# One layer of a hybrid diffusion model on one core: fewer gathers ticked in the latent finish, and its transposes queued later

## The chip, the core and the metric

The kernel runs on one core of a Trainium2 chip. TensorE (PE) multiplies matrices, with its weight loads listed as PEld; VectorE (DVE) and ScalarE (ACT) do the elementwise work, GpSimd (POOL) issues the indirect DMAs and a little arithmetic, and SyncE (SP) issues the plain loads and stores. The metric is the device time of one execution in microseconds, as the median of the runs.

## The reference

One layer is computed for 256 context tokens and 1024 latent tokens of width 1024. Attention and a recurrent mixer run side by side; their outputs go through one output projection and a gated residual, then a norm, and the result goes to an expert retrieval (PEER) with 16384 experts, of which every token takes 16 in each of 8 heads:

```python
    mix = jnp.concatenate([o_att, o_rnn.astype(o_att.dtype)], axis=-1)
    x = x + ga1 * jnp.einsum('bsm,md->bsd', mix, w_out)
    h2 = modulated_norm(x, g_ffn, sh2, sc2)
    x = x + ga2 * peer(h2, pq, psk, pu, pv)
...
        u = jnp.take(u_tab, eid, axis=0)
        act = jax.nn.gelu(jnp.einsum('td,thkd->thk', xb, u).astype(jnp.float32))
        vv = jnp.take(v_tab, eid, axis=0)
        return jnp.einsum('thk,thkd->td', (g * act).astype(vv.dtype), vv)
```

A final norm of every token ends it.

## The kernel before, in words

The tokens are ten tiles of 128: two of context, eight latent. The experts of six latent tiles are computed **densely**: every one of 128 groups of 128 experts is multiplied for all 768 tokens (the products u, lines 138 to 140), and what the retrieval did not choose is multiplied by zero. The other four tiles, two of context and two latent, take their experts by **gathers** in `mix` (lines 848 to 884): for each of a tile's 128 choices, POOL gathers 128 rows of `peer_u` (line 859) and DVE takes the dot product with the token (line 862), and for each again POOL gathers 128 rows of `peer_v` (line 873) and DVE adds them, weighted, to `acc` (line 879). One such step, called a row here, moves 128 by 1024 numbers of 4 bytes, 0.524 MB, and there are 1024 of them. A row waits for a free buffer: four serve it everywhere, three more in the dense part alone.

The stages run in this order: modulations and the context; the context's retrieval beside the latent projections, the recurrence and the rotation of queries and keys (lines 330 to 334); the latent attention, which begins with keys and queries cut in two halves (lines 398 to 414) for the scores (line 431); the latent **finish**, which is the output projection, residual and norm, tile by tile (lines 485 to 548); the **choose**, which finds the latent tiles' experts; the **spread**, in 96 blocks, which lays the chosen weights out over all experts (lines 697 to 706) while PE computes the u products of 44 groups ahead of the dense part ("early", 2112 matmuls of 384 columns); the **dense** part; and the last tiles' `final` (lines 835 to 845).

The rows are put between the other work by a clock. `tick(us)` is called after a piece of work and adds its microseconds; each time the clock has gone past a step the next row is emitted. The step is `F_STEP`, 1.9, up to the spread (others in some phases; none at all is emitted in the spread by its own tick), and `D_STEP`, 2.05, in the dense part. A scheduler then sets each engine's order from the place of emission and a simulated time of its own, so that a row can stand earlier than it was emitted, in any gap that it sees. In the dense part this is shut out: there each row's work is tied behind an add of that part (`paced`).

In the finish, `x` holds a tile's residual stream. Per tile PE makes two products of 512 columns (line 526, eight matmuls each), DVE multiplies by the gate and adds (lines 528 and 529), x is stored, ACT squares it (line 535), the root is taken with a step on POOL (lines 145 to 151), ACT scales x (line 537), and `to_columns` transposes it on PE (line 248) into the columns hh and hl that the experts' products take. In tiles that are gathered, f is transposed back (line 545) and stored.

## Time and profile before

| what | us |
|---|---|
| runs, median (lowest to highest of 3) | 3565.87 (3563.97 to 3566.43) |
| the profiled execution | 3568.34 |
| its span | 3566.5 |
| context, modulations | 0 to 365 |
| latent projection, recurrence, rotation, the context's retrieval | 245 to 534 |
| latent attention | 534 to 706 |
| latent finish | 706 to 887 |
| choose | 887 to 1177 |
| spread | 1222 to 1619 |
| what is left of the early products | 1619 to 1702 |
| dense part, to PE's last product | 1712 to 3521 |
| tail | 3521 to 3566.5 |

The stage's borders are read from the first and last instructions of its lines; stages overlap at them. The mean granted clock of the execution is 0.955 of full speed. A window's line gives each engine's busy time in it, with the number of instructions; a wait's line gives the time that an engine stood idle and the instruction whose end let it go on.

### The profile page before, as it was taken

The page shows a single profiled execution, that of the slowest core. Times are in us where ns is not written, and L with a number is a line of the kernel's source. Part 1 is how long each engine was busy: PE and PEld are TensorE (multiplying, and loading weights), DVE is VectorE, ACT ScalarE, POOL GpSimd, SP SyncE. Part 2 cuts the span into 40 slices and gives each one's busy share as a digit, 9 for nine tenths or more (in the row PEclk, how much of TensorE's full clock was granted, in tenths as well). Part 3 has the DMA queues.
Part 4 walks back from the last instruction along what each step waited for, and adds up shares of the span by engine and source line. Part 5 has one row for each costly group of instructions (what it writes and reads, how often), then busy time and mean ns, then how long its engine had stood idle before and what let it go on. Part 6 is the DMA issues. An engine that isn't in the chain of part 4 may idle for free.

```text
span 3566.5 us, 48580 instructions
## 1 busy us (share of the span) xinstructions
PE 3210.4 (90%) x16982; PEld 2704.1 (76%) x16982; DVE 3111.0 (87%) x6762; ACT 1429.9 (40%) x2242; POOL 1716.4 (48%) x1146
## 2 busy tenths in 40 slices
PE   7788868777999888888899999999999999999994
PEld 4477645433889877778788888878888887888884
DVE  4649989877999999993599999989999998999998
ACT  5734647523112344433333334333334333333432
POOL 0012451466521223443266666656666655666665
PEclk9799989988999999999999999999999999999997
DMA  8342652588621367795699999989999998999996
GB/s 331 136 152 82 216 206 83 185 276 290 219 89 31 122 199 214 233 315 185 242 325 337 337 330 334 340 308 335 329 328 339 327 340 290 332 327 336 335 339 223
DMA packets 349141, 918.19 MB, mean 257 GB/s; under 512 B 29144, under 2 KB 150104, under 8 KB 345824
## 3 DMA queue, kind: packets, MB, share of 16 engines
q0 software_dynamic: 147456, 536.94, 42.9%
q1 hardware_dynamic: 201440, 378.16, 30.8%
q8 instruction: 133, 2.18, 0.2%
q14 instruction: 112, 0.92, 0.1%
HBM read 834.48 MB, written 80.50 MB: 257 GB/s over the span
## 4 chain that ended last, share of the span: by engine, by line
PE 43%; DVE 22%; issue 8%; DMA 8%; POOL 3%; ACT 2%; SPq 0%; POOLq 0%; DVEq 0%; ACTq 0%
PE u L138 6%; PE u L140 6%; PE u L139 6%; PE rot L138 5%; PE rot L140 5%; PE rot L139 5%; DVE acc L879 3%; DVE row L862 3%; DMA row<-in_peer_u,eid 2%; PE res L138 2%; PE res L139 2%; PE res L140 2%; DMA row<-in_peer_v,eid 2%; DMA ad<-a 2%; DVE oh L699 1%
## 5 line engine op out<-in xcount | busy, mean ns | idle before, releaser
L859 POOL DMA_INDIRECT row<-in_peer_u,eid x512 | 749.9, 1465 | 603.3 <-DVE acc L879 201.7
L873 POOL DMA_INDIRECT row<-in_peer_v,eid x512 | 719.9, 1406 | 583.6 <-DVE acc L879 283.7
L138 PE MATMUL u<-hh,uh 128*128 128x384 f32 x2048 | 707.1, 345 | 22.4 <-ACT a L1028 22.4
L140 PE MATMUL u<-hh,ul 128*128 128x384 f32 x2048 | 705.6, 345 | 4.7 <-DVE ul L135 4.7
L139 PE MATMUL u<-hl,uh 128*128 128x384 f32 x2048 | 707.1, 345 | 0.0
L879 DVE SCALAR_TENSOR_TENSOR acc<-row,w,acc 128x1024 f32<-128x1024 f32 x508 | 663.4, 1306 | 25.2 <-DMA row<-in_peer_v,eid 23.7
L862 DVE SCALAR_TENSOR_TENSOR row<-row,h 128x1024 f32<-128x1024 f32 x512 | 623.0, 1232 | 62.8 <-DMA row<-in_peer_u,eid 62.6
L764 ACT ACTIVATE q<-rot 128x512 f32<-128x512 f32 x504 | 300.0, 597 | 523.5 <-PE rot L140 295.5
L138 PE MATMUL rot<-vh,ah 128*128 128x512 f32 x1024 | 409.1, 400 | 16.6 <-ACT q L764 16.1
L138 PEld LDWEIGHTS u<-hh,uh 128*128 128x128 f32 x2048 | 394.7, 193 | 29.8 <-ACT a L1028 23.8
L140 PEld LDWEIGHTS u<-hh,ul 128*128 128x128 f32 x2048 | 394.2, 192 | 9.7 <-DVE ul L135 5.1
L139 PE MATMUL rot<-vl,ah 128*128 128x512 f32 x1024 | 401.4, 392 | 0.0
L140 PE MATMUL rot<-vh,al 128*128 128x512 f32 x1024 | 400.6, 392 | 0.0
L139 PEld LDWEIGHTS u<-hl,uh 128*128 128x128 f32 x2048 | 394.6, 193 | 4.5
L765 DVE TENSOR_TENSOR acc<-q,acc 128x512 f32<-128x512 f32 x504 | 341.8, 686 | 45.4 <-ACT q L764 42.3
L140 PE MATMUL mm<-hh,wl 128*128 128x256 f32 (+2 forms) x848 | 289.7, 342 | 9.8 <-POOL wl L135 6.9
L138 PE MATMUL mm<-hh,wh 128*128 128x256 f32 (+2 forms) x848 | 286.3, 338 | 5.6 <-ACT wh L134 5.6
L139 PE MATMUL mm<-hl,wh 128*128 128x256 f32 (+2 forms) x848 | 284.3, 335 | 0.0
L134 ACT ACTIVATE uh<-u 128x1024 fp32r<-128x1024 f32 x128 | 135.8, 1061 | 331.3 <-PE u L139 302.0
L135 POOL TENSOR_TENSOR ul<-u,uh 128x1024 fp32r<-128x1024 f32 x44 | 122.8, 2791 | 277.8 <-ACT uh L134 237.5
L138 PEld LDWEIGHTS rot<-vh,ah 128*128 128x128 f32 x1024 | 193.4, 189 | 74.9 <-ACT q L764 36.7
L140 PEld LDWEIGHTS rot<-vh,al 128*128 128x128 f32 x1024 | 193.2, 189 | 41.5
(271 smaller groups left out, 5955.3 us busy)
## 6 DMA issues: line engine op xcount, KB each, us to landing
u<-in_ut SPq DMA_DIRECT2D x128, 512.0 KB
v<-in_peer_v SPq DMA_DIRECT2D x128, 512.0 KB
gd<-stg SPq DMA_DIRECT2D x12, 4096.0 KB
gt<-gd SPq DMA_DIRECT2D x64, 768.0 KB
w<-in_w_mod SPq DMA_DIRECT2D x24, 1024.0 KB
ad<-a SPq DMA_DIRECT2D x88, 192.0 KB
a<-ad SPq DMA_DIRECT2D x44, 384.0 KB
w<-in_w_query SPq DMA_DIRECT2D x32, 512.0 KB
```

The costliest lines, as they stand in the source:

```text
L134: A.activation(hi, src, AF.Copy)
L135: return (eng or V).tensor_tensor(lo, src, hi, op=OP.subtract)
L138: T.matmul(out, lhs[0], rhs[0], start=first, stop=False)
L139: T.matmul(out, lhs[0], rhs[1], start=False, stop=False)
L140: T.matmul(out, lhs[1], rhs[0], start=False, stop=last)
L699: V.tensor_tensor(oh.rearrange(four, j=2), o2.rearrange(four, j=2), pairs(gh, ts), op=OP.mult)
L764: A.activation(q, p, AF.Copy)
L765: tick(share / (2 * (N_DENSE - N_RES)), V.tensor_tensor(y, q, y, op=OP.add))
L859: G.indirect_dma_start(out=u, out_offset=None, in_=i["peer_u"], in_offset=bass.IndirectOffsetOnAxis(ap=eid[:, k:k + 1], axis=0))
L862: V.scalar_tensor_tensor(u, u, 1.0, h2, op0=OP.mult, op1=OP.mult, accum_out=act[:, j:j + 1])
L873: G.indirect_dma_start(out=v, out_offset=None, in_=i["peer_v"], in_offset=bass.IndirectOffsetOnAxis(ap=eid[:, k:k + 1], axis=0))
L879: V.scalar_tensor_tensor(acc, v, w[:, j:j + 1], acc, op0=OP.mult, op1=OP.add)
```

## The change

Three things. `D_STEP` goes from 2.05 to 2.0. In the latent finish the tick of 14 us a tile becomes 3 after each product and 2 at the end, 8 in all, so that 8 / 1.9 or about four rows are emitted a tile in the place of 14 / 1.9 or about seven. And a latent tile's norm, from the square to the transposes, moves into a function `normed` that is called after the next tile's products, with the transposes on PE tied behind the last of them (`issue_after`); x gets three buffers for it and f two. The context's finish has the same function without that tie, and its tick of 14 stays; f's second buffer is there too.

```diff
--- before.py
+++ after.py
@@ -51,7 +51,7 @@
 N_MORE = 3
 
 F_STEP = 1.9
-D_STEP = 2.05
+D_STEP = 2.0
 
 AFTER = 90.0
 STEP = {"spread": 1e9, "ret": 4.0, "early": 1.0}
@@ -507,13 +507,34 @@
         wk = pool(es, f"{pre}wk")
         ps = pool(es, f"{pre}po", 2, space=PSUM)
         xs = {}
+
+        def normed(t, x, behind):
+
+            ss = wk.tile([P, 1], F32, name="ss", bufs=2)
+            f = wk.tile([P, KD, P], F32, name="f", bufs=2)
+            A.activation(f.rearrange("p k t -> p (k t)"), x, AF.Square, accum_out=ss)
+            rs = rstd_of(ss, wk)
+            A.activation(x, x, AF.Copy, scale=rs)
+            hh, hl, us = dest(t)
+            with tc.issue_after(behind) if behind else nullcontext():
+                to_columns(ps, f, x, hh, hl, us, a2, b2, cond)
+                if t_0 + t in gt:
+                    h2 = wk.tile([P, D], F32, name="h2")
+                    for kk in range(2):
+                        p = ps.tile([P, 4, P], F32, name="tr")
+                        for k in range(4):
+                            T.transpose(p[:, k], f[:, kk * 4 + k], ident)
+                        A.activation(h2[:, kk * 512:(kk + 1) * 512], p.rearrange("p k t -> p (k t)"), AF.Copy)
+                    nc.sync.dma_start(h2d[t_0 + t], h2)
+
+        waiting = None
         for c0 in range(0, D, HW):
             if c0:
                 weights(c0)
             for t in tiles:
                 ts = slice(t * P, (t + 1) * P)
                 if c0 == 0:
-                    x = wk.tile([P, D], F32, name="x", bufs=2)
+                    x = wk.tile([P, D], F32, name="x", bufs=3 if lat else 2)
                     nc.sync.dma_start(x, x_in[ts, :])
                     xs[t] = x
                 x = xs[t]
@@ -523,29 +544,25 @@
                     p = ps.tile([P, W], F32, name="mm")
                     for k in range(KD):
                         oT = qT[:, k, ts] if k < 4 else gy[:, k - 4, ts]
-                        T.matmul(p, oT, wo[c0][:, k, wc], start=(k == 0), stop=(k == KD - 1))
+                        ins = T.matmul(p, oT, wo[c0][:, k, wc], start=(k == 0), stop=(k == KD - 1))
                     y = wk.tile([P, W], F32, name="y", bufs=2)
                     V.tensor_tensor(y, p, ga1[:, cols], op=OP.mult)
                     V.tensor_tensor(x[:, cols], y, x[:, cols], op=OP.add)
+                    if lat:
+                        tick(3)
                 if c0 + HW < D:
                     continue
                 nc.sync.dma_start(x1d[t_0 + t], x)
-                ss = wk.tile([P, 1], F32, name="ss", bufs=2)
-                f = wk.tile([P, KD, P], F32, name="f")
-                A.activation(f.rearrange("p k t -> p (k t)"), x, AF.Square, accum_out=ss)
-                rs = rstd_of(ss, wk)
-                A.activation(x, x, AF.Copy, scale=rs)
-                hh, hl, us = dest(t)
-                to_columns(ps, f, x, hh, hl, us, a2, b2, cond)
-                if t_0 + t in gt:
-                    h2 = wk.tile([P, D], F32, name="h2")
-                    for kk in range(2):
-                        p = ps.tile([P, 4, P], F32, name="tr")
-                        for k in range(4):
-                            T.transpose(p[:, k], f[:, kk * 4 + k], ident)
-                        A.activation(h2[:, kk * 512:(kk + 1) * 512], p.rearrange("p k t -> p (k t)"), AF.Copy)
-                    nc.sync.dma_start(h2d[t_0 + t], h2)
-                tick(14)
+                if not lat:
+                    normed(t, x, None)
+                    tick(14)
+                    continue
+                if waiting:
+                    normed(*waiting, ins.ins)
+                waiting = t, x
+                tick(2)
+        if waiting:
+            normed(*waiting, None)
 
 
     picks = {}
```

How many rows' work stands on DVE ahead of a place, counted in the order of the two programs:

| ahead of | before | after |
|---|---|---|
| the first cut of the latent queries (line 414) | 48 | 62 |
| the first gate multiply of the latent finish | 98 | 112 |
| the end of the latent finish (start of choose) | 180 | 200 |
| the end of choose | 210 | 223 |
| the first multiply of the dense part | 249 | 223 |
| the last add of the dense part | 1020 | 1012 |
| the program's end | 1024 | 1024 |

The retrieval weights of the two gathered latent tiles are combined on DVE (114 instructions); they stand behind the spread's last block before and inside the spread now. On PE, 414 of the early u products stand behind the last product of the spread before, 596 now.

DVE, the last rotations of the latent queries and keys and the halves of keys and queries that attention needs (kl, qs), before; L862 and L879 are rows:

```order
L332 TENSOR_TENSOR t_4236<-g,sinT 128x512
L862 SCALAR_TENSOR_TENSOR row,act<-row,h_4356 128x1024
L332 TENSOR_TENSOR t_4242<-g,sinT 128x512
L334 TENSOR_TENSOR qT<-qT,t_4236 128x512
L334 TENSOR_TENSOR qT<-qT,t_4242 128x512
L862 SCALAR_TENSOR_TENSOR row,act<-row,h_4356 128x1024
L399 TENSOR_TENSOR kl<-kcT,kh 64x256 x2
L399 TENSOR_TENSOR kl<-kT,kh 64x256 x4
L399 TENSOR_TENSOR kl<-kT,kh 64x512 x2
L414 TENSOR_TENSOR qs<-qT,qs 64x512 x3
```

and after, where rows are on L896 (or L879):

```order
L334 TENSOR_TENSOR qT<-qT,t_4242 128x512
L896 SCALAR_TENSOR_TENSOR acc<-row,w,acc 128x1024
L399 TENSOR_TENSOR kl<-kcT,kh 64x256 x2
L399 TENSOR_TENSOR kl<-kT,kh 64x256
L896 SCALAR_TENSOR_TENSOR acc<-row,w,acc 128x1024
L399 TENSOR_TENSOR kl<-kT,kh 64x256
L896 SCALAR_TENSOR_TENSOR acc<-row,w,acc 128x1024
L399 TENSOR_TENSOR kl<-kT,kh 64x256 x2
L896 SCALAR_TENSOR_TENSOR acc<-row,w,acc 128x1024
L399 TENSOR_TENSOR kl<-kT,kh 64x512 x2
L896 SCALAR_TENSOR_TENSOR acc<-row,w,acc 128x1024 x2
L414 TENSOR_TENSOR qs<-qT,qs 64x512 x4
```

The first qs stands behind 14 more rows in all; five rows have come among the kl, where there were none, and one right ahead of them stayed.

PE in the finish, before; the eight transposes tr are one tile's, mm the products, each product four matmuls with qT and four with gy:

```order
L526 MATMUL mm<-w,qT 128x512 x4
L526 MATMUL mm<-w,gy 128x512 x4
L526 MATMUL mm<-w,qT 128x512 x4
L248 MATMUL tr<-ident,x 128x128 x8
L526 MATMUL mm<-w,gy 128x512 x4
L526 MATMUL mm<-w,qT 128x512 x4
L526 MATMUL mm<-w,gy 128x512 x4
```

and after:

```order
L547 MATMUL mm<-w,qT 128x512 x4
L547 MATMUL mm<-w,gy 128x512 x4
L547 MATMUL mm<-w,qT 128x512 x4
L547 MATMUL mm<-w,gy 128x512 x4
L248 MATMUL tr<-ident,x 128x128 x8
L547 MATMUL mm<-w,qT 128x512 x4
```

A tile's transposes stood between the products of the next tile's second half, and stand behind the last of them now.

POOL at the program's end, before; a DMA row is a gather for the last tile, L147 a step of a final norm's root:

```order
L873 DMA row<-in_peer_v,eid_9939 128x1024 x4
L873 DMA row_31948<-in_peer_v,eid_9939 128x1024
L837 TENSOR_TENSOR acc_16235<-acc_16235,vh 128x1024
L837 TENSOR_TENSOR acc_16237<-acc_16237,vh 128x1024
L147 TENSOR_TENSOR rs_r<-rs_m,nhalf 128x1 x7
L1119 UNCONDITIONAL_BRANCH
```

and after:

```order
L854 TENSOR_TENSOR acc_16153<-acc_16153,vh 128x1024
L854 TENSOR_TENSOR acc_16155<-acc_16155,vh 128x1024
L890 DMA row<-in_peer_v,eid_9858 128x1024 x3
L147 TENSOR_TENSOR rs_r<-rs_m,nhalf 128x1
L890 DMA row<-in_peer_v,eid_9858 128x1024
L147 TENSOR_TENSOR rs_r<-rs_m,nhalf 128x1 x4
L890 DMA row<-in_peer_v,eid_9858 128x1024
L147 TENSOR_TENSOR rs_r<-rs_m,nhalf 128x1
L890 DMA row<-in_peer_v,eid_9858 128x1024
L147 TENSOR_TENSOR rs_r<-rs_m,nhalf 128x1
L1136 UNCONDITIONAL_BRANCH
```

The last six gathers went from ahead of the final norms to behind two tiles' gate multiplies (L854) and between the norms' roots: one root stands ahead of the fourth of them, five ahead of the fifth and six ahead of the last.

## Rows read from the trace of the kernel before

**Rows 1.** Windows: us; busy us (count) PE, PEld, DVE, ACT, POOL; PEclk; DMA; GB/s

```profile
450.00:534.00 84.00, 56.52 (x203) 38.52 (x203) 68.98 (x86) 36.83 (x57) 47.92 (x33) 0.87 0.59 208
...
706.00:887.00 181.00, 133.22 (x343) 64.70 (x344) 131.88 (x196) 54.60 (x105) 114.64 (x90) 0.86 0.83 282
...
887.00:1177.00 290.00, 266.80 (x1647) 255.92 (x1646) 281.86 (x1677) 60.46 (x101) 85.31 (x53) 0.96 0.36 112
...
1222.00:1619.00 397.00, 349.10 (x2813) 308.99 (x2813) 375.92 (x848) 172.87 (x210) 138.48 (x67) 0.95 0.76 232
...
1619.00:1650.00 31.00, 22.50 (x127) 22.18 (x125) 25.09 (x166) 11.74 (x16) 9.93 (x7) 0.89 0.92 286
...
1650.00:1700.00 50.00, 50.00 (x291) 50.00 (x290) 0.00 (x0) 10.64 (x17) 11.98 (x5) 1.00 0.27 90
...
2200.00:2800.00 600.00, 592.73 (x2876) 522.44 (x2876) 568.20 (x729) 230.69 (x350) 384.94 (x258) 0.99 0.91 331
...
3521.00:3566.50 45.50, 0.38 (x2) 0.00 (x0) 39.44 (x57) 11.04 (x20) 15.65 (x10) 0.55 0.39 149
```

**Rows 2.** Waits of PE and DVE, 450 to 535 us: total, times, longest

```profile
PE s L431 <- DVE qs L414: 20.7, 1, 20.7
...
DVE row L862 <- DMA row<-in_peer_u,eid: 6.8, 4, 3.4
```

**Rows 3.** Waits in the latent finish, 706 to 887 us

```profile
ACT x L537 <- DVE rs_r L151: 53.1, 8, 9.5
...
PE tr L248 <- ACT x L537: 46.2, 8, 17.9
...
DVE row L862 <- DMA row<-in_peer_u,eid: 28.0, 20, 4.0
...
DVE acc L879 <- DMA row<-in_peer_v,eid: 15.6, 12, 3.2
```

**Rows 4.** Line 528 in the finish: what DVE waited for before it

```profile
  PE mm L526: 0.5, 1
```

**Rows 5.** Lines of the finish: group | busy us, mean ns | idle before

```profile
L862 DVE SCALAR_TENSOR_TENSOR row<-row,h 128x1024 f32<-128x1024 f32 x43 | 54.3, 1268 | 28.2 <-DMA row<-in_peer_u,eid 28.0
...
L879 DVE SCALAR_TENSOR_TENSOR acc<-row,w,acc 128x1024 f32<-128x1024 f32 x38 | 48.8, 1284 | 16.2 <-DMA row<-in_peer_v,eid 15.6
```

**Rows 6.** Windows, two stretches of the spread

```profile
1250.00:1300.00 50.00, 44.06 (x372) 38.56 (x373) 48.98 (x135) 23.62 (x29) 10.64 (x4) 0.97 0.62 183
...
1500.00:1550.00 50.00, 43.66 (x332) 39.25 (x333) 45.81 (x63) 20.79 (x27) 23.34 (x15) 0.90 0.83 270
```

**Rows 7.** Waits of PE, spread to dense start, 1222 to 1720 us

```profile
PE g L703 <- DVE oh L699: 26.3, 16, 2.1
...
PE u L138 <- ACT a L1028: 17.2, 4, 8.5
...
PE res L138 <- ACT ah L134: 10.5, 1, 10.5
```

**Rows 8.** Waits of PE in the dense part, 1712 to 3525 us

```profile
PE rot L138 <- ACT q L764: 16.1, 9, 5.0
PE res L138 <- ACT ah L134: 14.9, 3, 10.5
```

**Rows 9.** Lines of DVE in the dense part

```profile
L862 DVE SCALAR_TENSOR_TENSOR row<-row,h 128x1024 f32<-128x1024 f32 x384 | 461.5, 1218 | 20.2 <-DMA row<-in_peer_u,eid 20.2
```

**Rows 10.** Timeline of DVE, tail: start us, us, engine, line

```profile
3542.78 1.21 DVE L838 TENSOR_TENSOR h<-acc,h 128x1024 f32<-128x1024 f32 x1
...
3550.11 1.28 DVE L842 SCALAR_TENSOR_TENSOR h<-h,rs_r,row 128x1024 f32<-128x1024 f32 x1
...
3559.95 2.48 DVE L842 SCALAR_TENSOR_TENSOR u<-u,rs_r,vh 128x1024 f32<-128x1024 f32 x2
```

**Rows 11.** Timeline of POOL, tail

```profile
3528.10 5.61 POOL L837 TENSOR_TENSOR acc<-acc,vh 128x1024 f32<-128x1024 f32 x2 [5.32 <-DMA vh<-modd]
...
3553.04 2.79 POOL L147 TENSOR_TENSOR rs_r<-rs_m,nhalf 128x1 f32<-128x1 f32 x2 [2.44 <-DVE rs_m L145]
```

## The prediction

> **What bounds the kernel now.** I read the windows first, by stage, then the waits of the engine that ends each stage, then the lines and the tail's timeline. The reader is to see that no one engine bounds the whole.
>
> Ahead of the latent attention PE stands 20.7 us at one place, until DVE has made the first halves of the queries [rows 2]. DVE is busy 69.0 of 84 us there [rows 1] and waits 6.8 us for gathered rows [rows 2]. DVE's queue is in order, so what stands on it ahead of these halves delays the attention.
>
> In the finish no engine is full: PE 133 of 181 us, DVE 132 [rows 1]. PE's one large wait is 46.2 us for scaled x, in eight pieces, one a tile [rows 3]. It looks like the stage's price and is not: before the gate multiplies, the first work on a tile's product, DVE waited for PE only once, 0.5 us [rows 4]. PE is ahead of DVE in spite of its stalls. DVE itself waits 43.6 us for gathered rows (28.0 and 15.6) [rows 3]. So DVE's in-order queue and the gathers feeding it set the pace: 81 rows in 181 us [rows 5], 2.2 us a row, where one row's work is 1.27 to 1.28 us [rows 5].
>
> Choose is DVE's: 281.9 of 290 us [rows 1]. In the spread both are near full, PE 349 of 397, DVE 376 [rows 1], and PE waits 26.3 us for one-hot tiles of DVE and 17.2 for ACT [rows 7]. What is left of the early products then runs at full PE with an idle DVE: 50.00 and 0.00 of 50 us [rows 1]. From there to the tail PE is the bound: 592.7 of 600 us in the window shown, DVE 568.2 [rows 1]; of its waits none as large as 6 us comes after the 10.5 at the start [rows 8]. The tail is DVE's and a chain: 39.4 of 45.5 us [rows 1].
>
> **The change part by part.** The counts are those of the table of rows ahead of places. The sum is made against the profiled execution, 3568.3 us, which is 2.5 above the median of the runs.
>
> *The way to the attention.* 14 more rows stand ahead of the first qs; 14 x 1.22 us (a row's dot product in the dense part, [rows 9]) is 17. Some of them fill DVE's idle time, 15 us in the last window before attention [rows 1]; eight of the 14 have already entered by the start of the rotation. If only what came later counts, it is 6 x 1.22 = 7. I take +10, from 0 (all in idle time) to +17.
>
> *The finish.* The tick falls from seven rows a tile to four, but the scheduler fills what it sees as gaps: 82 rows stand from the first gate multiply to the end before and 88 after. So the rows of this stage are not thinned. Six rows more at 2.2 us cost +13 at the gathers' pace, 7 at that of DVE. The transposes behind the next products take away up to 46.2 us of PE's waiting, but this was covered: DVE's wait for PE was 0.5 us. What can come of it is that x and f are free earlier and DVE's waits on the gathers overlap better; transfers ran at 282 GB/s here and at 331 in the dense part [rows 1], and 181 x 282 / 331 is 154, which no stage with this many dependences reaches; I allow a third of those 27 us. I take +6, from -10 to +13. The third x buffer only lets a load start earlier. What the second f buffer of the context's finish moves in the order lies ahead of the attention and is in the first term.
>
> *Choose, spread and the leftover products.* Choose holds 23 rows for 30; DVE is its bound, so 7 x 1.22 = -8.5. The spread held 39 rows, 47 us of DVE, and holds none, since the 223 emitted are used up; but the 114 instructions of the gathered tiles' weights, DVE's 25.1 us behind the spread [rows 1], move in: DVE has about 22 less to do in it. Does PE go faster then? A stretch without rows and one with them show the same PE: 44.06 and 43.66 of 50 us [rows 6]. The early products are a fixed number, and 182 more of them (596 for 414) come behind the spread; at 50 us for 291 [rows 1] they cost 31 us. The same 182 at the spread's PE share of 0.88 would free 36. So: -5 for this, and PE's 8.5 idle us in 1619 to 1650 [rows 1] go at best in part, which I leave in the bound. Choose and these: -13; because the 25 us of combining may not fit into DVE's 21 idle us of the spread, I take -11. Bounds: -30, if every row taken from the spread were worth its 0.8 us there, and +10 if the combining lies open and the choose keeps its length.
>
> *The dense part.* It holds 789 rows (1012 less 223) for 771 (1020 less 249), 18 more, since eight went behind its end. 18 x 1.22 = 22 us on DVE, which has 31.8 free us in 600 [rows 1], some 95 over the 1809. Covered, except where both are late at a time: PE's 16.1 us of waiting for ACT's rot copies [rows 8] shows such places. I take +3. If the cover were gone it is at most the transfers' price: 0.524 MB at 331 GB/s is 1.58 us a row, 18 of them +28 at most, and with one or two more late +32. The lower bound is 0, since nothing is removed.
>
> *The tail.* Twelve rows instead of four stand behind the last add, and the last tile's final comes last, on its own. The gathers for its last six rows stand on POOL behind two tiles' gate multiplies (5.6 us from 3528.1, [rows 11]), and the last two behind five and six roots; the corresponding ones of before end by 3555.8 [rows 11]. The last gather is then issued at about 3558 and lands some 3 to 4 us later (1.58 of transfer at least), 3562. Behind it come, in series, the row's 1.28 us, two of 1.21, the square and root and the scaling: from the add to the end of the scaling a final took 3542.78 to 3551.39 in the crowded tail [rows 10], some 6 alone. That ends at about 3571, against 3562.4 before (2.48 us from 3559.95, [rows 10]); the store behind is the same 4.1 us. I take +9, from +4 to +16.
>
> Sum: 10 + 6 - 11 + 3 + 9 = +17. 3568.3 + 17 = 3585.3 profiled, and 3583 on the median's footing.
>
> One rule bears on the dense term. There the row shows 331 GB/s at a busy share of 0.91 [rows 1]; whether that is a ceiling it cannot tell. The Trainium skill, "DMA: Bandwidth & Descriptors", section Specifications, gives about 358 GB/s as the limit of memory for one core. By the page 18 rows more, 9.4 MB over 1809 us or 5 GB/s, fit and cost nothing; by the row taken as a ceiling they cost the 28 above. No run here shows the 358.
>
> **The rivals.**
>
> *Faster, about 3535:* DVE's rows are what everything ahead of the dense part pays for. 26 fewer rows stand ahead of its first multiply, and at 1.22 us that is 32. For it: DVE waited for ahead of the attention and in the spread [rows 2, 7], full in choose. In terms: the first 0, finish -10, spread and choose -30, dense 0, tail +9: -31, 3535. Against it: the equal PE shares of rows 6, and that its gains lie in the spread, while PE's products only move behind it. It decides where the spread's blocks are paced by DVE and not by both.
>
> *No difference, about 3566:* the 14 early rows fit into DVE's gaps, the finish keeps its pace, and the -9 of choose pays for the +9 of the tail.
>
> *Slower still, about 3612:* the dense part is full of transfers. 0.91 [rows 1] is all there is, so each added row lengthens it by 1.58 us, +32 in the place of my +3. For it: DVE waits 20.2 us there for gathered rows [rows 9]. Against it: PE, the bound, names no transfer among its large waits [rows 8]. It decides once the rows fall behind the adds to which they are tied.
>
> That the change does not do what it says (no four rows a tile) is part of the forecast, not a rival.
>
> **How the numbers follow.** A measurement here tells about 0.2% from nothing, 7 us. My forecast has 0.46, the faster rival 0.28, no difference 0.14, the slower one 0.12. The likeliest time is 3583; its own range, the terms' bounds not all at one end, is 3566 to 3603. Slower by over 0.2% is 0.46 + 0.12 = 0.58, faster 0.28, within 0.14. The range of 8 in 10 takes in the two other cases to about their middles: 3533 to 3610, with some 0.12 left out below and 0.06 above.
>
> **What would show it.** In the changed profile: PE's wait for the first qs over 25 us and attention starting about 10 us later (first term); the finish 181 us or more, though PE's wait for scaled x falls below 10 (second); choose shorter by 8, the spread shorter by 20 to 30 and the leftover products longer by 31 (third); PE in the dense windows still at 0.98 or above (fourth); PE's last product to the end 52 to 61 us for 45 (fifth). I am wrong if the dense part begins more than 15 us earlier than 1712, or if its length of 1809 grows by over 10.

## The result, and the profile after

The changed kernel takes 3624.3 us (median of 3 runs, 3620.5 to 3629.0) for 3565.9: a ratio of 1.0166, with an interval of 1.0143 to 1.0189. It is slower, as forecast, but by 58 us where 17 were forecast, and outside the range. Its profiled execution took 3629.0 us with a span of 3626.9, 60.4 above that of before, and this is the execution that the readings below are from.

Borders read from the first and the last instruction of a line in each trace give the span by stage. "Score" is the first score of the latent attention (line 431), "gate" the last gate multiply of the latent finish, "choose" the last instruction of the choose, "spread" its last one-hot tile, "dense" the first multiply of the dense part, "add" its last add.

| us | to score | to gate | to choose | to spread | to dense | dense to last add | tail |
|---|---|---|---|---|---|---|---|
| before | 533.9 | 332.1 | 311.3 | 439.1 | 94.0 | 1815.1 | 41.0 |
| after | 556.8 | 338.7 | 313.7 | 402.2 | 121.2 | 1836.6 | 57.7 |
| difference | +22.9 | +6.6 | +2.4 | -36.9 | +27.2 | +21.5 | +16.7 |

Two of the columns are cut at other places than the forecast's terms. By the first product of the finish (705.9 us before, 733.2 after) and its last hl (887.6 and 921.2), as the forecast had it, the latent attention is 4.4 us longer, the finish 6.3 longer and the choose 1.7 shorter.

The windows of the kernel after at its own borders answer to [rows 1] (columns as there):

```profile
450.00:557.00 107.00, 71.13 (x265) 49.16 (x263) 92.07 (x105) 51.96 (x75) 58.86 (x43) 0.89 0.63 220
...
725.00:920.00 195.00, 138.91 (x372) 66.04 (x369) 142.86 (x206) 57.88 (x111) 120.18 (x98) 0.86 0.85 290
...
920.00:1210.00 290.00, 266.62 (x1643) 255.42 (x1642) 279.63 (x1684) 57.36 (x99) 86.49 (x52) 0.95 0.34 109
...
1245.00:1615.00 370.00, 323.85 (x2661) 282.89 (x2660) 344.88 (x955) 180.70 (x214) 66.11 (x23) 0.94 0.62 183
...
1615.00:1660.00 45.00, 41.95 (x245) 41.02 (x242) 0.00 (x0) 8.92 (x13) 12.41 (x7) 1.00 0.75 223
...
1660.00:1710.00 50.00, 48.45 (x280) 48.20 (x279) 0.00 (x0) 12.90 (x20) 15.49 (x7) 1.00 0.37 111
...
2222.00:2822.00 600.00, 575.20 (x2758) 504.94 (x2757) 551.96 (x708) 220.24 (x334) 363.57 (x257) 0.98 0.89 321
...
3565.00:3626.90 61.90, 1.31 (x6) 0.75 (x4) 47.11 (x65) 11.29 (x20) 23.32 (x18) 0.55 0.45 159
```

The reader is to see three things. The spread is 37 us shorter, but PE is busy for no larger share of it (323.9 of 370; 349.1 of 397 before), so what it has not done stands behind, where DVE is idle in two windows on end. The dense window has 575 busy us of PE for 593; over the whole dense part PE stands idle for 43.8 of 1831 us, for 26.6 of 1809 before. And the tail is 62 us for 45.

The place that [rows 2] showed, then the gather waits of DVE from 365 us to the score, in the kernel after:

```profile
PE s L431 <- DVE qs L414: 25.2, 1, 25.2
...
DVE row L879 <- DMA row<-in_peer_u,eid: 11.3, 7, 4.5
...
DVE acc L896 <- DMA row<-in_peer_v,eid: 8.5, 8, 1.5
```

The finish, answering to [rows 3]:

```profile
PE tr L248 <- ACT x L517: 49.2, 8, 21.8
...
DVE acc L896 <- DMA row<-in_peer_v,eid: 31.6, 19, 4.0
...
DVE row L879 <- DMA row<-in_peer_u,eid: 20.4, 19, 3.9
```

PE waits as long for scaled x as before, 49.2 us for 46.2: the transposes were queued later, and the wait stayed. DVE waits 52.0 us for gathers in this window (725 to 920 us; 2.4 of them lie ahead of the finish's first product) instead of 43.6.

PE's waits in the dense part, answering to [rows 8]:

```profile
PE res L138 <- ACT ah L134: 28.5, 7, 10.0
PE u L140 <- DVE ul L135: 12.7, 3, 5.4
PE rot L138 <- ACT q L781: 10.2, 12, 3.6
```

The wait for ah has gone from 14.9 us to 28.5, and that for ul from 4.7 to 12.7; that for ACT's rot copies (q) has fallen from 16.1 to 10.2.

DVE's waits for loads in the dense part, before and then after:

```profile
DVE row L862 <- DMA row<-in_peer_u,eid: 20.2, 8, 5.0
DVE a L784 <- DMA a<-ad: 7.0, 5, 2.4
```

```profile
DVE a L801 <- DMA a<-ad: 19.6, 9, 7.0
DVE row L879 <- DMA row<-in_peer_u,eid: 19.0, 13, 3.9
```

The tail, first POOL's and then DVE's timeline, answering to [rows 10, 11]:

```profile
3572.60 4.63 POOL L854 TENSOR_TENSOR acc<-acc,vh 128x1024 f32<-128x1024 f32 x2 [3.68 <-DMA vh<-modd]
...
3603.98 1.91 POOL L890 DMA_INDIRECT row<-in_peer_v,eid  x1 [1.78 <-DVE rs_m L145]
...
3606.95 1.45 POOL L890 DMA_INDIRECT row<-in_peer_v,eid  x1 [0.19 <-issue]
```

```profile
3613.35 1.28 DVE L896 SCALAR_TENSOR_TENSOR acc<-row,w,acc 128x1024 f32<-128x1024 f32 x1 [2.55 <-DMA row<-in_peer_v,eid]
...
3617.00 1.22 DVE L855 TENSOR_TENSOR h<-acc,h 128x1024 f32<-128x1024 f32 x1
...
3619.50 0.15 DVE L145 TENSOR_SCALAR rs_m<-ss 128x1 f32<-128x1 f32 x1 [1.27 <-ACT acc L857]
...
3621.03 1.29 DVE L859 SCALAR_TENSOR_TENSOR h<-h,rs_r,vh 128x1024 f32<-128x1024 f32 x1
```

The last gather is issued at 3606.95, behind the sixth root, lands for a sum at 3613.35 after 2.55 us of DVE's waiting, and the last tile's final follows alone, to 3622.3.

### The profile page after: what moved, and what is told of

Its sections match the earlier page's. It is cut to its first block, busy times and chain, and to the rows that moved or that the text cites. A ratio compares the mean times of both kernels' runs of the same rounds, so it can differ in the third digit from the quotient of the medians.

```text
span 3626.9 us, 48603 instructions
## 1 busy us (share of the span) xinstructions
PE 3225.8 (89%) x16982; PEld 2704.2 (75%) x16982; DVE 3102.6 (86%) x6762; ACT 1433.6 (40%) x2245; POOL 1676.9 (46%) x1146
## 4 chain that ended last, share of the span: by engine, by line
PE 40%; DVE 27%; issue 12%; DMA 11%; POOL 7%; ACT 3%; SPq 1%; POOLq 0%; DVEq 0%; ACTq 0%
PE u L140 5%; PE u L138 5%; PE u L139 5%; PE rot L138 4%; DVE row L879 4%; PE rot L140 4%; PE rot L139 4%; DMA row<-in_peer_u,eid 3%; POOL row L890 3%; DVE acc L896 3%; DMA row<-in_peer_v,eid 3%; POOL row L876 2%; PE res L138 2%; PE res L140 2%; PE res L139 2%
## 5 line engine op out<-in xcount | busy, mean ns | idle before, releaser
L876 POOL DMA_INDIRECT row<-in_peer_u,eid x512 | 728.9, 1424 | 640.2 <-DVE row L879 226.6
L890 POOL DMA_INDIRECT row<-in_peer_v,eid x512 | 708.9, 1385 | 474.4 <-DVE acc L896 237.3
L140 PE MATMUL u<-hh,ul 128*128 128x384 f32 x2048 | 702.5, 343 | 22.0 <-DVE ul L135 12.7
L896 DVE SCALAR_TENSOR_TENSOR acc<-row,w,acc 128x1024 f32<-128x1024 f32 x508 | 656.1, 1291 | 44.9 <-DMA row<-in_peer_v,eid 43.1
L879 DVE SCALAR_TENSOR_TENSOR row<-row,h 128x1024 f32<-128x1024 f32 x512 | 622.9, 1230 | 65.1 <-DMA row<-in_peer_u,eid 64.9
L138 PE MATMUL rot<-vh,ah 128*128 128x512 f32 x1024 | 408.1, 399 | 11.2 <-ACT q L781 10.2
L138 PEld LDWEIGHTS u<-hh,uh 128*128 128x128 f32 x2048 | 392.1, 191 | 12.7 <-ACT a L1045 7.2
L135 DVE TENSOR_TENSOR vl<-v,vh 128x1024 fp32r<-128x1024 f32 x128 | 155.8, 1218 | 120.0 <-ACT vh L134 119.9
```

Of the source, the lines that this page charges most:

```text
L135: return (eng or V).tensor_tensor(lo, src, hi, op=OP.subtract)
L138: T.matmul(out, lhs[0], rhs[0], start=first, stop=False)
L140: T.matmul(out, lhs[1], rhs[0], start=False, stop=last)
L876: G.indirect_dma_start(out=u, out_offset=None, in_=i["peer_u"], in_offset=bass.IndirectOffsetOnAxis(ap=eid[:, k:k + 1], axis=0))
L879: V.scalar_tensor_tensor(u, u, 1.0, h2, op0=OP.mult, op1=OP.mult, accum_out=act[:, j:j + 1])
L890: G.indirect_dma_start(out=v, out_offset=None, in_=i["peer_v"], in_offset=bass.IndirectOffsetOnAxis(ap=eid[:, k:k + 1], axis=0))
```

## The experiments

The table has the stages of each kernel as above, from one profiled execution each; the ratios stand with the runs. Single executions differ: the twelve kernels of this document that have 48 rows ahead of the score, as before has, begin it between 531.6 and 538.4 us. The dense part takes 1814.2 to 1820.0 us in the five kernels of the two tables with step 2.05, and 1830.6 to 1836.8 in the four with 2.0.

| us | to score | to gate | to choose | to spread | to dense | dense | tail |
|---|---|---|---|---|---|---|---|
| context_f_single | 534.7 | 326.6 | 309.7 | 418.6 | 101.8 | 1830.6 | 57.9 |
| before_context_f_double | 556.2 | 334.7 | 309.6 | 431.0 | 96.7 | 1815.3 | 41.0 |
| before_step_200 | 536.5 | 332.2 | 310.5 | 442.7 | 94.8 | 1831.1 | 35.3 |
| before_ticks_8 | 533.7 | 326.6 | 310.2 | 416.1 | 104.5 | 1817.7 | 88.7 |
| before_ticks_8_step_200 | 537.1 | 326.2 | 309.6 | 418.1 | 103.7 | 1836.8 | 57.0 |
| norm_moved_alone | 537.6 | 324.4 | 307.6 | 442.8 | 83.2 | 1814.2 | 40.9 |
| latent_buffers_alone | 532.1 | 335.2 | 311.1 | 441.8 | 94.8 | 1820.0 | 41.2 |
| norm_moved_more_ahead | 534.3 | 322.5 | 314.0 | 461.4 | 101.8 | 1796.8 | 35.3 |

### One buffer undone: context_f_single

```diff
-            f = wk.tile([P, KD, P], F32, name="f", bufs=2)
+            f = wk.tile([P, KD, P], F32, name="f", bufs=2 if lat else 1)
```

> The changed kernel with f in the context's finish back at one buffer (two in the latent finish). The row counts ahead of the first query half and of the first gate multiply go back to those of before (48 and 98, for 62 and 112). Theory A (the reshuffled order before the attention is a term of its own, made by that buffer and worth what the first score's start shows, 533.9 to 556.8 us): attention starts near 534 and the median falls by about 23, to about 3601. Rival B (the rows only move; what is not done ahead of the attention is late in the finish and the choose): attention starts near 534, but the dense part still starts near 1732 and the median stays within 8 of 3624.

The median was 3586.8 us, a ratio of 1.0061 (1.004 to 1.0083) to the kernel before. The attention starts at 534.7 and the dense part at 1691.4, where the changed kernel had 1732.6. Theory A: the buffer is a term of its own, and dearer than expected, some 37 us of the 58 (1.0166 / 1.0061 = 1.0104). Of the difference between the two profiled executions, 22.1 us lie ahead of the score and 12.1 between it and the last gate multiply.

### The same buffer alone: before_context_f_double

```diff
-                f = wk.tile([P, KD, P], F32, name="f")
+                f = wk.tile([P, KD, P], F32, name="f", bufs=1 if lat else 2)
```

> The kernel before with the second buffer of f in the context's finish and nothing else. Theory A (this buffer alone reorders the time ahead of the attention and what follows, and is the largest part of the change's loss): first score at 555 to 560 for 533.9, the dense part starts 20 to 40 later, the median is 20 to 40 above that of before. Rival B (it costs only together with the moved norm or the fewer ticks): median within 10 of before.

The ratio was 1.0067 (1.0042 to 1.0093), about +23 us. The score starts at 556.2 and the dense part 17.8 later than before, a little under the 20 of theory A, which holds otherwise. The window from 365 us to the score, before and then in this kernel:

```profile
365.00:533.90 168.90, 130.72 (x485) 90.32 (x485) 146.34 (x169) 94.11 (x126) 88.84 (x62) 0.92 0.65 218
```

```profile
365.00:556.20 191.20, 142.71 (x506) 97.93 (x505) 165.59 (x184) 96.40 (x129) 103.30 (x73) 0.87 0.66 223
```

DVE is busy for 19.3 us more and idle for 3.0 more (25.6 for 22.6): the added rows did not fill idle time. They are 14 weighted sums of `peer_v` rows, 29 for 15, at 1.33 us each in this window. The waits of PE and of DVE ahead of the score, in this kernel:

```profile
PE s L431 <- DVE qs L414: 24.4, 1, 24.4
...
DVE row L862 <- DMA row<-in_peer_u,eid: 12.1, 8, 3.6
...
DVE acc L879 <- DMA row<-in_peer_v,eid: 9.1, 7, 2.6
```

DVE's waits for gathers are 21.2 us; up to 534 us they were 8.6 before. Alone the buffer costs 23, with the rest of the change 37. Where the other 14 arise is not shown by a run. The tables point to two places: to the last gate multiply the buffer adds 2.6 us alone and 12.1 with the rest, and spread and leftover products, which it shortens by 5.4 together when alone, become 3.0 longer (context_f_single against the kernel after), though some 18 rows fewer stand in the spread.

### Is it the rows' work? context_f_double_thin_rows

```diff
+                    hw = 32 if t == 0 and k < 16 else D
-                    V.scalar_tensor_tensor(u, u, 1.0, h2, op0=OP.mult, op1=OP.mult, accum_out=act[:, j:j + 1])
+                    V.scalar_tensor_tensor(u[:, :hw], u[:, :hw], 1.0, h2[:, :hw], op0=OP.mult, op1=OP.mult, accum_out=act[:, j:j + 1])
```

> The kernel before with the context's f doubled, where the first score started at 556.2; the first 16 dot products of the first gathered tile (16 rows, 1.22 us each) take 32 of their 1024 elements and leave the rest out; their gathers stay. Theory A (what makes attention late is the time of the 14 rows more on DVE's in-order queue): the first score starts 12 to 20 earlier, 536 to 544. Rival B (the other order of the recurrence and rotation, or the wait for the gathers, makes it late): it starts within 6 of 556.

The score started at 553.5, 2.7 earlier, in the one execution of this kernel; by the number that is rival B. PE waits 23.1 us for the same queries, and DVE's waits for gathers have grown to 26.3:

```profile
365.00:553.50 188.50, 140.35 (x506) 98.40 (x506) 154.87 (x187) 96.24 (x128) 106.62 (x77) 0.88 0.69 235
```

```profile
PE s L431 <- DVE qs L414: 23.1, 1, 23.1
...
DVE row L863 <- DMA row<-in_peer_u,eid: 16.0, 12, 2.9
...
DVE acc L880 <- DMA row<-in_peer_v,eid: 10.3, 9, 2.4
```

It does not settle the question, since the rows ahead of the score did not stay the same: there are 67 for 62 now. DVE is busy 10.7 us less than in before_context_f_double and idle 8.0 more. So taking work from DVE brought attention forward by little here, because more rows and waits for them came in its place; what the same 62 rows with thin sums would give is not shown.

### Neither sums nor bytes: before_tiny_rows and context_f_double_tiny_rows

```diff
+                hw = 32 if t == 0 and k < 32 else D
-                G.indirect_dma_start(out=u, out_offset=None, in_=i["peer_u"],
+                G.indirect_dma_start(out=u[:, :hw], out_offset=None, in_=i["peer_u"] if hw == D else i["peer_u"].rearrange("n (h d) -> (n h) d", h=32),
...
-                    V.scalar_tensor_tensor(u, u, 1.0, h2, op0=OP.mult, op1=OP.mult, accum_out=act[:, j:j + 1])
+                    V.scalar_tensor_tensor(u[:, :hw], u[:, :hw], 1.0, h2[:, :hw], op0=OP.mult, op1=OP.mult, accum_out=act[:, j:j + 1])
```

The gathers of `peer_v` and their sums are cut in the same way.

> The kernel before with the same tiny first 64 rows, as the other end of that comparison. Both theories: first score earlier than 533.9. Under A the rows' price ahead of the attention is what this run gains, up to 30 us; under B it gains under 10.

> The kernel before with the context's f doubled (first score at 556.2), and the first 64 rows of the first gathered tile, those that stand ahead of the attention, gather and use 32 of 1024 columns (out of the table read as short rows; the rest of their sums is left out): neither their transfers nor their work on DVE is left to speak of. Theory A (the rows make attention late, by DVE's waits for their gathers: 21.2 us for 8.6 before, where the work alone was shown not to): first score within 6 of that of before with the same tiny rows. Rival B (the order of recurrence and rotation itself is worse with that buffer): first score 10 or more later than that of before with the same tiny rows.

Both kernels ran once. The first missed under either theory: the score started at 569.5, later than with whole rows. In the second it started at 582.0, 12.5 later still, which is rival B by the number. The window from 365 us to the score with tiny rows (the one of before stands above):

```profile
365.00:569.50 204.50, 138.52 (x484) 94.00 (x484) 142.62 (x235) 99.07 (x132) 129.16 (x108) 0.86 0.40 136
```

POOL's count is the thing to see: 108 instructions for 62, against less DVE work (142.6 us for 146.3) and less of the DMA engines (0.40 for 0.65). Some 45 more gathers stand ahead of the score, presumably since the scheduler finds room for more of the shorter rows. 98 gathers in these 204.5 us are 2.1 us each, near the 2.2 a row of the finish, though 64 of them move a thirty-second of the bytes. So attention can go late by the number of gathers ahead of it, with less work for DVE and fewer bytes. That is as far as it is settled: with the second buffer the two tiny kernels stand 12.5 us apart, and whether this is six more gathers or the other order of the recurrence these runs don't tell.

### The closer step alone: before_step_200

```diff
-D_STEP = 2.05
+D_STEP = 2.0
```

> The kernel before with D_STEP 2.0 alone: no row stands behind the last dense add (4 before), so 775 rows stand beside the dense part for 771. Theory A (a row beside the dense part is not covered by its work; it costs about 1.2 us or more, and the closer step makes PE wait for late adds): the dense part of 1809 us grows by 10 to 20, the tail shrinks by 5, the median is 3571 to 3582. Rival B (rows beside the dense part are covered): dense grows by under 4, the tail shrinks by 5 to 8, the median is 3558 to 3564.

The ratio was 1.0022 (1.0008 to 1.0036), median 3578.0 for 3568.3. Dense grew by 16.0 and the tail fell by 5.7. DVE's waits in the dense part of this kernel, and the line of its adds (count, ns, first and last start):

```profile
DVE row L862 <- DMA row<-in_peer_u,eid: 36.4, 20, 5.6
...
DVE acc L765 <- ACT q L764: 34.0, 33, 3.3
...
L765 DVE TENSOR_TENSOR acc<-q,acc x504: 674/686/737, 1771.7 to 3547.8; 128x512 f32<-128x512 f32 x168
```

Theory A. DVE waits 36.4 us for gathered rows where it waited 20.2 [rows 9]. This execution is the longest of the kernel's ten (3584.9), but the four kernels at step 2.0 agree on the dense part. Four rows more made 16 us, so their number is hardly the cause; the next pair tests that.

### Fewer ticks, with either step: before_ticks_8_step_200 and before_ticks_8

```diff
                     V.tensor_tensor(x[:, cols], y, x[:, cols], op=OP.add)
+                    if lat:
+                        tick(3)
...
-                tick(14)
+                tick(2 if lat else 14)
```

With `D_STEP` 2.0 in the first and 2.05 in the second.

> The kernel before with the ticks of 3, 3 and 2 and D_STEP 2.0, but the norm where it was and one buffer for f. 223 rows stand ahead of the dense part for 249, 1012 ahead of its end; up to the choose the order is that of before. Theory A (dense term and tail belong to the moved rows): attention starts at 534, dense grows by about 20, the tail by about 15, spread and leftover products together by about 0: median 3590 to 3605. Rival B (they belong to the moved norm or to the context's order): dense and tail each within 5 of before, median 3560 to 3575.

> The kernel before with the ticks of 3, 3 and 2, and D_STEP 2.05 as before: 223 rows ahead of the dense part, 774 beside it (with step 2.0 and no fewer ticks it was 775), 27 behind its last add. Theory A (the dense part's length follows the step, that is how close the rows stand, not their number; what stands behind costs 1.4 to 2.1 us a row): dense 1815 within 5, from the last add to the end 41 + 23 x 1.4 to 2.1 = 73 to 89, start of dense 16 to 20 earlier than before: median 3580 to 3600. Rival B (the number of rows beside the dense part sets its length): dense 1827 or more.

The first had 3591.6 us, 1.0073 (1.0049 to 1.0097), the second 3603.6, 1.0119 (1.0098 to 1.014). In the second the dense part is 1817.7 us with 774 rows, as at 2.05 with 771 (1815.1) and not as at 2.0 with 775 (1831.1): the length follows the step, theory A. The last add of that kernel stands at 3508.8:

```profile
L767 DVE TENSOR_TENSOR acc<-q,acc x504: 675/691/2818, 1745.3 to 3508.8; 128x512 f32<-128x512 f32 x168
```

From there the 27 rows behind it take 88.7 us to the end. Four took 41.0, twelve 57.7, none 35.3: between 1.4 and 2.1 us a row. The second run's median is 3.6 us above theory A's range. In the first theory A holds too, but for the spread and the leftover products, which are 11 us shorter together where it had about 0. In both the price of the rows that were taken from ahead of the dense part is paid behind its last add or by a closer step, and the start of the dense part is only some 19 us earlier for it (1691.1 for 1710.4).

### The moved norm alone: norm_moved_alone and latent_buffers_alone

The first is the changed kernel with these lines back:

```diff
-D_STEP = 2.0
+D_STEP = 2.05
...
-            f = wk.tile([P, KD, P], F32, name="f", bufs=2)
+            f = wk.tile([P, KD, P], F32, name="f", bufs=2 if lat else 1)
...
-                    if lat:
-                        tick(3)
...
-                tick(2)
+                tick(14)
```

The second is the kernel before with the buffers alone:

```diff
-                    x = wk.tile([P, D], F32, name="x", bufs=2)
+                    x = wk.tile([P, D], F32, name="x", bufs=3 if lat else 2)
...
-                f = wk.tile([P, KD, P], F32, name="f")
+                f = wk.tile([P, KD, P], F32, name="f", bufs=2 if lat else 1)
```

> The moved norm alone: transposes tied behind the next tile's last product, x with three and latent f with two buffers; the context's f has one buffer, the tick is 14 a tile and D_STEP 2.05, as before. Theory A (PE's wait for scaled x in the finish was covered by DVE's queue): PE's wait of 46 us changes, but the finish stays within 5 us of 181 and the median within 7 of 3566. Rival B (PE's wait was on the path): the finish is 15 or more us shorter and the median under 3555.

> The kernel before with x at three and f at two buffers in the latent finish; the norm stays where it was, the context's f has one. Theory A (the moved norm's gain of 9 us in the finish comes from its place behind the next products): finish as before, 147 us from the first gate multiply to the last, median within 5 of before. Rival B (it comes from the buffers): finish 138 to 141, median 8 to 15 below that of before.

The moved norm had 3554.2 us for 3568.3, a ratio of 0.9967 (0.9953 to 0.9982): 12 us faster by the ratio, 14 by these medians, the one complete version here that beats both kernels. The buffers alone gave 1.0001 (0.9987 to 1.0014) and 148.8 us from the first gate multiply to the last, theory A, so the gain is that of the place. PE's wait in the finish, and the gate multiplies with DVE's wait for PE, in the moved norm:

```profile
PE tr L248 <- ACT x L517: 38.9, 7, 16.0
...
L549 DVE TENSOR_TENSOR y<-mm,ga x16: 680/684/693, 724.4 to 862.0; 128x512 f32<-128x512 f32 x16
...
  PE mm L547: 0.3, 1
```

PE still waits 38.9 us and DVE's wait for PE is 0.3: of the 46 only 7 went, where the prediction had the wait fall below 10. From the first gate multiply (724.4) to the last (862.0) it is 137.6 us for 147.0 before. The gain came with DVE's waits for gathers, 39.4 us for 43.6, and a stretch from the spread to the dense part that is 11 shorter; neither theory had that second half, and no run here explains it. The result lies between the two expectations: the finish is 9 us shorter, where A had under 5 and B 15 or more, and the median is just under B's bound.

### More rows ahead of the dense part: norm_moved_more_ahead

On top of the moved norm:

```diff
-D_STEP = 2.05
+D_STEP = 2.1
...
-AFTER = 90.0
+AFTER = 130.0
```

> The moved norm alone (context's f with one buffer, tick 14), with AFTER 130 for 90 and D_STEP 2.1 for 2.05: 40 more rows are emitted beside the early products that are left, where DVE stood idle for 63 us, so 289 rows stand ahead of the dense part for 249; 735 beside it for 771 and none behind its last add for four. Theory A (rows beside the dense part and behind it are dear, those beside the leftover products are covered): dense starts within 8 of the 1695.6 of the moved norm alone, is 5 to 15 shorter and the tail 5 shorter; median 3530 to 3548. Rival B (the leftover products lose what the dense part gains): dense starts 15 or more later, median 3550 to 3565.

The ratio was 1.0006 (0.9992 to 1.002). Dense is 17.4 shorter than with the moved norm alone and the tail 5.6, but the dense part starts 38.4 later: 40 rows at 0.96 us. The window from the spread's last tile to it, and the adds of the dense part:

```profile
1632.00:1734.00 102.00, 64.70 (x354) 63.12 (x352) 66.30 (x214) 22.18 (x33) 55.27 (x40) 0.82 0.90 303
...
L780 DVE TENSOR_TENSOR acc<-q,acc x504: 674/684/725, 1787.1 to 3530.8; 128x512 f32<-128x512 f32 x168
```

Rival B, with a median 3 us above its range. PE is busy for 64.7 of 102 us in that window and DVE for 66.3; in the same stretch of the moved norm alone (1612.4 to 1695.6 us) they are busy for 69.1 and 15.3 of 83.2. The DMA engines' share is 0.90 for 0.55 there. The longest waits of PE and of ACT from 1600 to 1734 us:

```profile
PE u L138 <- ACT a L1043: 27.5, 2, 24.8
```

```profile
ACT L1043 <- DMA ad<-a: 18.8, 1, 18.8
```

The rows there are not covered, though DVE had stood idle beside the leftover products: PE stands still for ACT's activations, and ACT, by the profile, for the store of an earlier one, which is a transfer. A step of 2.1 makes the dense part 1796.8 (with fewer rows beside it, 735), of 2.05 1814 to 1820, of 2.0 1831 to 1837, over the kernels of the two tables.

### What the closer step pays for: four kernels with part of a row's cost

All leave the adds and their ties alone and change only what a row in the dense part moves or sums. step_200_half_sums, on before_step_200:

```diff
+                    hw = D // 2 if cur[0] == "dense" else D
-                    V.scalar_tensor_tensor(u, u, 1.0, h2, op0=OP.mult, op1=OP.mult, accum_out=act[:, j:j + 1])
+                    V.scalar_tensor_tensor(u[:, :hw], u[:, :hw], 1.0, h2[:, :hw], op0=OP.mult, op1=OP.mult, accum_out=act[:, j:j + 1])
...
-                        V.scalar_tensor_tensor(acc, v, w[:, j:j + 1], acc, op0=OP.mult, op1=OP.add)
+                        V.scalar_tensor_tensor(acc[:, :hw], v[:, :hw], w[:, j:j + 1], acc[:, :hw], op0=OP.mult, op1=OP.add)
```

step_200_half_rows gathers the half alone as well, from `peer_u` and in the same way from `peer_v`:

```diff
-                G.indirect_dma_start(out=u, out_offset=None, in_=i["peer_u"],
+                G.indirect_dma_start(out=u[:, :hw], out_offset=None, in_=i["peer_u"] if hw == D else i["peer_u"].rearrange("n (h d) -> (n h) d", h=2),
```

> The kernel before with D_STEP 2.0, and in the dense part DVE takes only the first half of each gathered row's elements (512 of 1024; the rest of the dot product and of the sum is left out); the gathers move the same bytes. Theory A (the closer step costs because DVE, at 96 to 98 of 100 us, falls behind the adds): the dense part, 1831 us from the first multiply to the last add, falls to 1805 or less and PE's waits for DVE and ACT go. Rival B (it costs because of the transfers: 0.91 to 0.96 of the DMA engines busy): dense stays within 6 of 1831.

> As the run with half sums, and the gathers of the dense part move half the bytes too (512 of 1024 columns, out of the tables read as rows of half the length, so that the rows are those of other experts). Theory A (DVE): the same dense part as with half sums, within 5. Rival B (transfers): another 20 or more us less than with half sums.

Half the sums made the kernel slower, 1.0289 (1.0255 to 1.0322), with a dense part of 1929.6 us. Half the sums and half the bytes gave 0.9976 (0.9956 to 0.9995) and 1811.7. A window of 200 us in the dense part, and DVE's wait for the activations a (the first kernel), then the same window of the second:

```profile
2800.00:3000.00 200.00, 189.80 (x918) 168.06 (x917) 138.89 (x222) 72.75 (x109) 87.13 (x82) 0.97 0.87 322
...
DVE a L784 <- DMA a<-ad: 128.7, 32, 8.2
```

```profile
2800.00:3000.00 200.00, 196.41 (x972) 174.48 (x972) 152.31 (x254) 77.51 (x117) 102.79 (x93) 1.00 0.71 229
```

With DVE down to 138.9 of 200 us the dense part is longer, not shorter, which neither expectation had: DVE waits for loads (128.7 us for a, 7.0 before), at 0.87 of the DMA engines, and PE 78.7 us for the ah that are made of them. With half the bytes the engines are at 0.71, PE is busy for 196.4 us, and its wait for ah is 18.4; the part is 118 us shorter than with half the sums alone, rival B. DVE's share of busy time is thus not by itself what bounds the dense part. But the order around the adds had changed in both, so a cleaner pair followed, in which DVE reads the gathered half of a `peer_v` row twice and so keeps its whole work, at either step:

```diff
-                G.indirect_dma_start(out=v, out_offset=None, in_=i["peer_v"],
+                half = cur[0] == "dense"
+                G.indirect_dma_start(out=v[:, :D // 2] if half else v, out_offset=None, in_=i["peer_v"] if not half else i["peer_v"].rearrange("n (h d) -> (n h) d", h=2),
...
+                        a2_ = acc.rearrange("p (h d) -> p h d", h=2)
+                        V.scalar_tensor_tensor(a2_, v[:, None, :D // 2].to_broadcast([P, 2, D // 2]), w[:, j:j + 1], a2_, op0=OP.mult, op1=OP.add)
```

> The kernel before with D_STEP 2.0; in the dense part the gathers of peer_v move half their bytes (512 columns, of other experts) and DVE reads that half twice, so its work is whole; a quarter of the rows' bytes is gone. Theory A (the closer step costs by transfers that come too late, 36.4 us of DVE's waits for gathers against 20.2 at 2.05): dense 1831 falls to 1815 or less. Rival B (it costs by DVE's work, 98 of 100 us): dense stays within 5 of 1831.

> The kernel before, step 2.05, with the same halved gathers of peer_v in the dense part. Theory A: dense falls little, to 1800 to 1815, so that the two steps come within 6 of each other. Rival B: within 5 of 1815, and the two steps stay 12 or more apart.

The dense part took 1822.1 us at step 2.0 and 1811.1 at 2.05; the ratios were 1.0 (0.9984 to 1.0015) and 0.9996 (0.9979 to 1.0013). The window from 2800 to 3300 us at step 2.0, whole and with the halved rows, and DVE's wait for rows in the second:

```profile
2800.00:3300.00 500.00, 477.72 (x2290) 415.39 (x2289) 454.93 (x583) 181.48 (x276) 312.52 (x211) 0.98 0.89 320
```

```profile
2800.00:3300.00 500.00, 481.59 (x2313) 420.28 (x2312) 459.25 (x589) 182.74 (x279) 321.98 (x216) 0.99 0.77 264
```

```profile
DVE row L862 <- DMA row<-in_peer_u,eid: 28.5, 16, 4.8
```

A quarter of the rows' bytes less took 9 of the 16 us at step 2.0 and 4 at 2.05; the two steps stand 11 apart instead of 16. The 9 is clear of the 6 us by which kernels at one step differ, the 4 is not. So transfers are a part of it and, as far as these runs tell, not all. It was expected to be one or the other, and neither expectation holds; what the rest is stays open.

## Why the prediction was wrong

**By terms and by edits.** The forecast missed by 43 us: 18.5 in the dense part, 12.9 on the way to the attention, 7.7 in the tail, 3.7 from choose to the leftover products, 0.6 in the finish. By edits the dearest is the context's buffer, which alone returns 37 of the 58 us.

**The way to the attention: +10 forecast, +22.9 measured.** The step that failed is "some of them fill DVE's idle time". I priced the 14 rows at a dot product's 1.22 us and took off what DVE had idle, and I counted the eight that had entered by the start of the rotation as free; but the rotation itself started 18 us later (502.2 for 484.2). With the buffer alone DVE's idle time ahead of the score did not shrink, it grew by 3.0 us, and its busy time grew by 19.3 of the 22.3 us: the rows cost their whole work, as weighted sums of 1.33 us and not dot products, and some waiting on top, 1.6 us a row in all. Whether their gathers' pace would set the same price is not separated from it: with thin or tiny rows more of them came ahead, and attention stayed late or went later. PE's wait of 25.2 us at the first score, only 4.5 more than before, was the wrong place to look for the size: the lag was there already.

**The second context buffer** was in the list of the change, and I put all that it moves into that term. That holds for 22 us. The run that undoes it alone returns 37 of the 58, and the rest lies behind the score, 12 of it ahead of the last gate multiply. I saw none of that, and why the buffer costs more with the rest of the change than alone stays open.

**The finish: +6 forecast, +6.6 measured** to the last gate multiply, with the attention in it, and +6.3 by the forecast's own borders. That this is near is luck in part. The step that the transposes behind the next products take away PE's waiting failed: 49.2 us of it are left, and 38.9 in the moved norm alone. DVE's own wait for PE, 0.3 us, supports the step that this wait is covered; but no run took the wait away, so none tests it. The 9 us that I had allowed for x and f being free earlier are what the moved norm gave alone (137.6 for 147.0), and the whole kernel was 12 faster. Whether that gain outlasts the rest of the change is not clear: 0.9967 and 1.0073 would make 1.004, and context_f_single, which has both, is at 1.0061 (1.004 to 1.0083).

**Choose, spread and leftover: -11 forecast, -7.3 measured** (+2.4, -36.9, +27.2). The reasoning that rows taken from the spread give back little holds by these three: the spread gave 37 and the leftover took 27. That the sum is near is luck in part. From the last hl to its last instruction the choose holds 29 rows for 31 in the traces, not seven fewer, and gave 1.7 us where I had 8.5; spread and leftover gave 9.7 where I had 2.5. And I read [rows 6] wrongly: PE is busy for the same share in both stretches, but it does 372 products in the one without rows and 332 in the other, at a granted clock of 0.97 and 0.90. The spread's own products were 213 in the one without rows and 176 in the other, so PE did get on with them; the forecast came near because the early products are a fixed number and what the spread leaves of them stands behind it.

**The dense part: +3 forecast, +21.5 measured.** The step that failed is "it has 31.8 free us in 600": I summed the rows' number and covered it by DVE's idle share. Here 2.0 for 2.05 alone costs 16 us with only four rows more, and 774 rows at 2.05 cost 3. What the step sets is how close the rows stand, and with a closer step something comes too late: with the step alone DVE's waits for them were 36.4 us for 20.2; in the changed kernel itself these are 19.0, and its waits for the activations a, loaded by SP, 19.6 for 7.0. The loss is not even: past the start most stretches of 50 us have PE busy for over 48 in both kernels; in the kernel after it falls to 41 to 46 in each of 2383 to 2483, 2583 to 2683 and 3033 to 3133 us, in that before to 44 to 46 in 2360 to 2410 and 2910 to 3010. I should have priced the constant that the change edits and not the count that follows from it.

The rival with +32 had its sign and a part of its mechanism: a quarter of the rows' bytes less gives 9 of 16 back. But 0.91 of the engines was not all there is: single stretches of 50 us in the kernel before have 0.99, at 372 GB/s (1933 to 1983 us). With the 358 GB/s of the Trainium skill, "DMA: Bandwidth & Descriptors", section Specifications, the added transfers would have cost nothing. The three dense windows of the kernel after, at 321 to 334 GB/s, stay below that figure as means, while single stretches pass it, here with 373 GB/s (2033 to 2083 us); so the trace does not show 358 as a ceiling, against what I wrote, that no run shows the figure. The part was longer all the same: a mean below a limit did not show here that transfers cost nothing.

**The tail: +9 forecast, +16.7 measured.** The mechanism was right, gathers behind roots on POOL and a final on its own, and the size was off: the last gather was issued at 3606.95, 41 us behind PE's last product, where I had 37, and its sum came 6.4 us after the issue began, where I had 3 to 4. Eight more rows to the end cost 2.1 us each, and +9 had made that 1.1.

**The faster rival** said that rows ahead of the dense part are paid for at 1.22 us. They are at about 0.75 (19 us for 26 rows, fewer ticks) to 0.96 (38 us for 40, more ahead). So its mechanism is real. It lost because the same rows cost more at the other end, 1.4 to 2.1 behind the last add, because the step was closed to keep that number at twelve, and because the context's buffer made the dense part start 41 us later than it does without it (1732.6 for 1691.4).

## What to carry to other kernels

Price a constant that sets how close background work stands by its own edge, not by the work it adds in sum: free time in an average does not cover a closer spacing where each piece is tied to a place. Where background work stands on an engine ahead of work that others wait for, do not take it to fill idle time: read whether the engine's idle time shrinks, and count the work in full until it does. And a buffer added in a stage that the change is not about can move the order of every stage behind it, so each such edit is worth a run of its own: here it cost 37 us, and everything else in the change 22.

## What the runs showed that I had not expected

Less work for DVE made the dense part longer: with half the sums DVE was busy for 139 of 200 us and the part took 1929.6 us for 1831.1, with long waits for loads. And making 64 rows next to free drew attention 36 us later: 94 rows stood ahead of it then, for 48.
